# Output products of the context rows moved into the last attention units of a two-layer transformer kernel

## The chip, the core and the metric

The kernel runs on one core of one Trainium2 chip. The metric is device microseconds of one launch, as the median of several runs. Five engines work side by side, each through its own instruction list in order: PE (matrix products and transposes; PEld is its weight load), DVE (vector), ACT (scalar functions), POOL (a second vector engine) and SP, which here only issues DMAs. They wait for one another by semaphores.

## The reference, cut to what matters

Two layers over 1024 tokens and 256 context rows, width 1024. The change touches the end of the first (even) layer: the differential attention B, the gates, the output product with its residual, and the normalised input of the second layer.

```python
qa, ka, va, qb, kb, vb, g = _split(h @ w_in, EVEN_SPLITS)          # tokens; the context likewise from hc
ya = _window_gqa_sink(...)                                          # attention A, done before stage B
s = einsum('bqhte,bkhte->bhtqk', q, k) * e ** -0.5                  # attention B, 4 heads, two score maps t
p = softmax(s); a = p[:, :, 0] - lam * p[:, :, 1]
yb = rmsnorm(einsum('bhqk,bkhe->bqhe', a, v), b_subln_g) * (1.0 - lam_init)
y = concatenate([ya, yb], -1) * silu(g)
x = x + gate * (y @ w_out)                                          # 1024 token rows
xc = xc + gate_c * (yc @ w_out)                                     # 256 context rows, same w_out
h, gate = _modulate(x, ...); hc, gate_c = _modulate(xc, ...)        # second layer starts with a norm of each row
```

## The kernel before

Every product of activations and weights is made of three matmuls (`mm3`, L304 to L306): both operands are split into a high and a low part, and high x high, high x low and low x high are summed in PSUM. Splitting a tile is a rounding copy on ACT (the high part) and a subtraction on DVE or POOL (the low part, L214 and L218).

Stage B (`mark("B")` up to `mark("outE")`) has 20 units: 4 heads, and in each head five pairs of 128-row query blocks, the context pair (8, 9) first and then four token pairs. I number them 0 to 19; units 0, 5, 10 and 15 are the short context ones. A unit has three parts. `b_scores`: score matmuls (L906, into `sps`), their evacuation on DVE with a running minimum (L407), the exponential on ACT (L914), and the mix of the two score maps, on POOL for the first row block (L924 and the sums) and on DVE for the second (L927). `b_values`: transposes of the mixed maps (L955), a split on ACT and DVE (`phb`, `plb`), and products with V (L418 to L420). `b_norm`: after every second token unit a transposed RMS norm of the head's output (L977 to L1002) and, at a head's end, a store to DRAM (`ote`, L1000 and L1005).

`pipeline` lays these steps out at positions in units (values about 1.7 units after their scores, norms about 2.3 to 2.7) and between steps lets a filler emit other work: per unit of position the filler may emit `FILL_B` = 5.0 "us" of it, by the numbers that the filler's generator yields. That generator is `gates()`: eight gate projections (`gate_proj`: 12.8 us of yields each, PE products of `hE` with `whi` and `wlo`, a tanh on ACT and ten DVE steps, L396 and L398, then a store `gte`), and then the split of the eight 128-row tiles of the output weights (`fill_out_weights`, L847 to L855, 5.0 each; `woraw` is the loaded tile, with two buffers, `woE` the split weights). These tiles lie where `hE` and the gates' buffers lay, so they begin when the gates are done. What is left after the last unit is emitted by `fill.drain()`. Within reach, a list scheduler then orders the instructions of each engine, so the emission order is the frame and not the last word.

Stage outE goes over ten row blocks, context blocks 8 and 9 first, then 0 to 7. For each, `y_get` loads attention output and gate (`o_in`, `g_in`, three buffers each), multiplies and splits them (`yh`, `yl`); `out_half` makes 24 matmuls for each half of the columns and then two DVE steps, times the gate row (`t_o`, L1036) and plus the residual (`xn`, L1037). Each pair of blocks is normalised (`norm_rows`), and one block later transposed into the second layer's input `hO` (`emit_h`). The gate row `gate_e` has one buffer: the context's is loaded for blocks 8 and 9, the tokens' for the rest.

Of the kernel before, what the change touches and what calls it, by code (L numbers as in the profile page):

```python
# [9 lines left out]
F32 = mybir.dt.float32  # L10
# [22 lines left out]
SM_N = 332  # L33
FILL_A, FILL_B, FILL_D, FILL_M = 5.0, 5.0, 4.3, 5.0
S_BUFS_A, S_BUFS_B, S_BUFS_D, S_BUFS_M, K_BUFS_B, Q_BUFS_B = 11, 7, 12, 6, 1, 3
# [7 lines left out]
WO_RAW, Y_BUFS = 1, 3  # L43
Q_BUFS_D, WO_V, WO_Y, YL_V = 2, 2, 5.0, 1
POOL_MIX, POOL_Q = (0,), (8,)
# [51 lines left out]
def body(nc, tc, I, out, dbg=None):  # L97
# [82 lines left out]
    def f32(ap):  # L180
        return ap.bitcast(F32)
# [661 lines left out]

    def fill_out_weights(rp, wo, src, bufs=2):
        for kt in range(NK):
            raw = rp.tile([P, D], F32, tag="wada", name="woraw", bufs=bufs)
            SY.dma_start(raw, src[:, kt * D:(kt + 1) * D])  # L847
            for c in range(2):
                cs_ = slice(c * 512, (c + 1) * 512)
                A.copy(wo[c][0][:, kt], raw[:, cs_])  # L850
                eng = V if WO_V and kt % WO_V == c else G
                tt(eng, wo[c][1][:, kt], raw[:, cs_], f32(wo[c][0][:, kt]), ALU.subtract)
            yield WO_Y

# [3 lines left out]
    def y_part(t, src, gsrc, half, b):  # L858
        op, (yh, yl) = t
        ks = slice(4 * half, 4 * half + 4)  # L860
        bs = slice(b * P, (b + 1) * P)
        o, g = (op.tile([P, 4, P], F32, tag=x, name=x, bufs=Y_BUFS) for x in ("o_in", "g_in"))
        SY.dma_start(o, src[half][:, :, bs].rearrange("k p t -> p k t"))
        SY.dma_start(g, gsrc[half][:, :, bs].rearrange("k p t -> p k t"))
        V.scalar_tensor_tensor(o, o, 0.5, g, ALU.mult, ALU.mult)
        A.copy(yh[:, ks], o)  # L866
        tt(V if YL_V and half == YL_V - 1 else G, yl[:, ks], o, f32(yh[:, ks]), ALU.subtract)


# [3 lines left out]
    with ExitStack() as st:  # L873
# [134 lines left out]
        def gates():  # L1008
            with ExitStack() as gs:
                gp = pool(gs, "gateE", 2, side="right")  # L1010
                yield from items([w_item(W, [I["w_e"][18 + i]], lambda w, i=i: gate_proj(
                    gp, w, h, CHUNKS, GTE[i // 4][i % 4], T, True)) for i in range(8)])
            hE.close()
            with ExitStack() as gs:
                wo_box.append(out_weights(stW, "woE", "right"))
                wo_box.append(pool(stW, "yE", 1, side="right"))
                ad = pool(gs, "adaE", 2, side="right")
                yield from fill_out_weights(ad, wo_box[0], I["w_out_e"])

# [6 lines left out]
        fill.drain()  # L1026
    wo, yp = wo_box


    def out_half(op, y, wo, x, gate, xn, c, kts):  # L1030
        cs_ = slice(c * 512, (c + 1) * 512)
        ps = mm_ps()
        for i, kt in enumerate(kts):
            mm3(ps, y[1][0][:, kt], y[1][1][:, kt], wo[c][0][:, kt], wo[c][1][:, kt], i == 0, i == NK - 1)
        t = op.tile([P, 512], F32, tag="t", name="t_o")
        V.tensor_tensor(t, ps, gate[:, cs_], ALU.mult)  # L1036
        V.tensor_tensor(xn[:, cs_], x[:, cs_], t, ALU.add)  # L1037

# [7 lines left out]
    with ExitStack() as st:  # L1046
        op = pool(st, "outE", 1, side="left")
        kts = list(range(NK))

        def y_get(b):  # L1050
            t = y_load(yp)
            for half in range(2):
                y_part(t, OTE, GTE, half, b)
            return t

        order = [8, 9] + list(range(8))
        ys = {8: y_get(8)}
        gate = None
        late = []

        def emit_h(blocks, xns):
            run(h_cols(op, xns, 1, 1 if blocks[0] == 8 else 0, blocks[0] * P, h2, width=256))

        for gi in range(0, 10, 2):
            blocks, xns, x_in = order[gi:gi + 2], [], []
            if gi in (0, 2):
                gate = op.tile([P, D], F32, tag="gate", name="gate_e", bufs=1)
                gate_load(gate, 1 if gi == 0 else 0)
            for i, b in enumerate(blocks):
                xn = op.tile([P, D], F32, tag="xn", name="xn", bufs=3)  # L1070
                SY.dma_start(xn, I["x_o"][b * P:(b + 1) * P] if b < 8 else I["ctx"][(b - 8) * P:(b - 7) * P])
                nb = order[gi + i + 1] if gi + i + 1 < 10 else None
                if nb is not None:
                    ys[nb] = y_get(nb)
                else:
                    w_kd0 = Wp.load([I["w_o"][3]])
                y = ys.pop(b)
                for c in range(2):
                    out_half(op, y, wo, xn, gate, xn, c, kts)
                    if late and c == EMIT_C:  # L1080
                        emit_h(*late.pop(0))
                if b < 8:
                    SY.dma_start(X1[b], xn)
                xns.append(xn)
            norm_rows(op, xns)
            late.append((blocks, xns))
# [418 lines left out]
    with ExitStack() as st:  # L1505
# [14 lines left out]
        for b in range(8):  # L1520
# [8 lines left out]
            for c in range(2):  # L1529
                out_half(op, y, wo, x, gate2, xn, c, kts)  # L1530
                junk = op.tile([P, 512], BF16, tag="junk", name="junk2", bufs=2)
# [82 lines left out]
```

## Time and profile before

| what | us |
|---|---|
| median of 3 runs (lowest, highest) | 1668.4 (1663.4, 1669.59) |
| the profiled execution's own time | 1664.82 |
| its span | 1663.0 |
| PE busy in the span | 1582.6 (95%) |
| DVE busy | 1085.4 (65%) |
| ACT busy | 777.3 (47%) |
| POOL busy | 540.3 (32%) |

The profiled execution lies 1.8 us above its span and 3.6 us below the median. PE's busy time counts a matmul to its modelled end, so that neighbours overlap: how much work stands in a stretch is better counted from matmuls times the distance of their starts. The windows of the trace give busy time by stretch; I cut them where PE passes from one kind of work to the next: 478.9 us (scores of unit 0 done), 717.1 (of unit 16), 762.5 (of unit 19, the last), 822.7 (first transposes of normalised rows in outE) and 910.6 (first product of the second layer).

### The profile page before, as it was taken

The numbers are of one execution on the slowest core, as the hardware profiler recorded it, in microseconds if no ns is written. First come the engines' busy times: TensorE is split into PE (matmuls) and PEld (weight loads), VectorE is DVE, ScalarE is ACT, GpSimd is POOL, SyncE is SP. The second block draws the span as 40 slices with busy tenths as digits, with TensorE's granted clock in tenths as the row PEclk, the third lists the DMA queues.
The fourth block names the chain that finished last, engine by engine and source line by source line (L and its number), as shares of the span: only waits on it lengthen the run. The fifth ranks groups of instructions, "written<-read, shape, count | busy, mean of one in ns | idle before, by whom it ended". The sixth has DMA issues, their size and how long they took to land. (4 is left out here: it accounts for less than half of the span.)

```text
span 1663.0 us, 26799 instructions
## 1 busy us (share of the span) xinstructions
PE 1582.6 (95%) x9266; PEld 1330.1 (80%) x9266; DVE 1085.4 (65%) x2954; ACT 777.3 (47%) x1580; POOL 540.3 (32%) x713
## 2 busy tenths in 40 slices
PE   6988999999998999998999998999999999999997
PEld 3676767888877878887687897989788887888886
DVE  4674128878759887888776456352777757666576
ACT  5443107766646655666323323222566646554321
POOL 0465025555534433333323203120333314322211
PEclk9999999999999999999999999999999999999999
DMA  7447663252253332223853514666855445321452
GB/s 294 172 124 256 223 213 105 83 159 81 76 203 101 112 102 99 90 90 117 247 164 133 171 45 134 192 203 210 211 166 166 137 130 183 101 77 64 140 190 83
DMA packets 147375, 242.99 MB, mean 146 GB/s; under 512 B 10252, under 2 KB 93096, under 8 KB 145064
## 3 DMA queue, kind: packets, MB, share of 16 engines
q1 hardware_dynamic: 142328, 227.91, 44.1%
q10 hardware_dynamic: 4576, 11.54, 1.8%
q0 software_dynamic: 336, 1.84, 0.3%
q8 instruction: 73, 1.20, 0.3%
q14 instruction: 62, 0.51, 0.1%
HBM read 163.50 MB, written 77.74 MB: 145 GB/s over the span
## 5 line engine op out<-in xcount | busy, mean ns | idle before, releaser
L304 PE MATMUL mmps<-hE,whi 128*128 128x512 f32 (+1 forms) x408 | 148.6, 364 | 1.2 <-DVE gg L396 1.2
L218 POOL TENSOR_TENSOR wlo<-wraw,whi 128x256 fp32r<-128x256 f32 x120 | 92.2, 803 | 173.0 <-ACT whi L251 173.0
L306 PE MATMUL mmps<-hE,wlo 128*128 128x512 f32 (+1 forms) x408 | 146.4, 359 | 0.0
L305 PE MATMUL mmps<-hE,whi 128*128 128x512 f32 (+1 forms) x408 | 146.1, 358 | 0.0
L914 ACT ACTIVATE sB_t<-sB_t,mB 128x1280 f32<-128x1280 f32 (+1 forms) x80 | 95.5, 1194 | 57.1 <-DVE sB_t L407 50.6
L906 PE MATMUL sps<-kb,qb 128*128 128x512 f32 (+1 forms) x416 | 107.9, 361 | 4.5 <-DMA kb<-kb 2.3
L924 POOL TENSOR_SCALAR sB_t<-sB_t,cB 128x256 f32<-128x256 f32 x84 | 38.7, 482 | 156.3 <-DVE cB L920 74.8
L1449 POOL TENSOR_SCALAR sM_t<-sM_t,sM 128x1280 f32<-128x1280 f32 x32 | 43.3, 1353 | 137.4 <-DVE sM L1448 106.4
L304 PEld LDWEIGHTS mmps<-hE,whi 128*128 128x128 f32 x408 | 77.3, 189 | 11.4 <-issue 2.1
L407 DVE TENSOR_SCALAR_CACHE_REDUCE sB_t<-sps,mB 128x512 f32<-128x512 f32 (+1 forms) x128 | 78.2, 612 | 12.5 <-PE sps L906 9.7
L306 PEld LDWEIGHTS mmps<-hE,wlo 128*128 128x128 f32 x408 | 77.2, 189 | 9.9 <-issue 0.8
L305 PEld LDWEIGHTS mmps<-hE,whi 128*128 128x128 f32 x408 | 77.2, 189 | 9.2 <-issue 0.8
L906 PEld LDWEIGHTS sps<-kb,qb 128*128 128x128 f32 x416 | 69.4, 191 | 16.9 <-DVE sB_t L407 5.9
L1347 POOL TENSOR_SCALAR sD_t<-sD_t,sD 128x640 f32<-128x640 f32 (+1 forms) x64 | 48.5, 780 | 90.0 <-DVE sD L1344 37.1
L218 POOL TENSOR_TENSOR rot<-rot,csE 128x256 f32<-128x256 f32 x52 | 41.3, 816 | 109.0 <-DVE rot L331 105.2
L305 PE MATMUL mmps<-hO,whi 128*128 128x512 f32 (+1 forms) x192 | 75.0, 390 | 1.7 <-POOL hO L214 1.6
L304 PE MATMUL mmps<-hO,whi 128*128 128x512 f32 (+1 forms) x192 | 75.5, 393 | 0.0
L306 PE MATMUL mmps<-hO,wlo 128*128 128x512 f32 (+1 forms) x192 | 74.4, 388 | 0.0
L784 ACT ACTIVATE sA_t<-sA_t,mA 128x640 f32<-128x640 f32 (+2 forms) x80 | 59.6, 745 | 31.8 <-DVE sA_t L407 29.2
L218 POOL TENSOR_TENSOR yl<-o_in,yh 128x256 fp32r<-128x256 f32 x36 | 34.0, 966 | 121.9 <-ACT yh L866 121.7
L221 ACT CAST phm<-tps 128x512 fp32r<-128x512 f32 x80 | 45.7, 584 | 51.6 <-PE tps L1476 51.3
L794 POOL TENSOR_SCALAR sA_t<-sA_t,eA 128x640 f32<-128x640 f32 (+2 forms) x80 | 56.1, 724 | 37.9 <-DVE eA L792 14.6
(437 smaller groups left out, 5208.1 us busy)
## 6 DMA issues: line engine op xcount, KB each, us to landing
wraw<-w_e SPq DMA_DIRECT2D x26, 512.0 KB
wada<-w_ada_e SPq DMA_DIRECT2D x24, 512.0 KB
wada<-w_ada_o SPq DMA_DIRECT2D x24, 512.0 KB
wraw<-w_o SPq DMA_DIRECT2D x22, 512.0 KB
qb<-qk SPq DMA_DIRECT2D x76, 128.0 KB
qd_t<-qd SPq DMA_DIRECT2D x32, 256.0 KB
qk<-hl SPq DMA_DIRECT2D x10, 512.0 KB
vb<-vh SPq DMA_DIRECT2D x10, 512.0 KB
```

Of the source, the lines that this page charges most:

```text
L218: eng.tensor_tensor(out_[:, cs_], a[:, cs_], b[:, cs_], op)
L221: A.copy(dst_hi, src)
L304: T_.matmul(ps, lh, rh, start=first, stop=False)
L305: T_.matmul(ps, lh, rl, start=False, stop=False)
L306: T_.matmul(ps, ll, rh, start=False, stop=last)
L407: V.tensor_scalar(dst, ps, -scale, prev, ALU.mult, ALU.min, accum_out=acc)
L784: A.activation(St[:, :nl + L], St[:, :nl + L], AF.Exp, bias=mx, scale=-1.0, accum_out=ssum[:, i:i + 1])
L794: G.tensor_scalar(Ps[i][:, :nl + L], Ps[i][:, :nl + L], e[:, i:i + 1], 1.0, ALU.mult, ALU.mult)
L906: T_.matmul(ps[:, :n], Q[:, t, hl, i * P:(i + 1) * P], K[:, t, c0:c0 + n], start=hl == 0, stop=hl == 1)
L914: A.activation(St[:, :ncol], St[:, :ncol], AF.Exp, bias=mx, scale=-1.0, accum_out=s0g[:, si:si + 1] if t == 0 else ssum)
L1347: G.tensor_scalar(Ps[i][:, :w_], Ps[i][:, :w_], ssum[:, i:i + 1], 1.0, ALU.mult, ALU.mult)
L1449: G.tensor_scalar(St, St, ssum, 1.0, ALU.mult, ALU.mult)
```

## The change

`FILL_B` goes from 5.0 to 6.0, so the gates are used up after fewer units. The output weights are yielded at 2.5 instead of 5.0 each (`WO_YE`), so they are emitted under the last units. The generator then goes on: it takes a pool `outC`, loads the context's gate row and residual rows, fetches `y` for blocks 8 and 9 and emits their four `out_half` (5.12 us of yields each). Stage outE keeps blocks 0 to 7 only, with the context rows' norm at its start. The gate row is still one buffer (tag `gate`), now in `outC`.

```diff
-FILL_A, FILL_B, FILL_D, FILL_M = 5.0, 5.0, 4.3, 5.0
+FILL_A, FILL_B, FILL_D, FILL_M = 5.0, 6.0, 4.3, 5.0
-Q_BUFS_D, WO_V, WO_Y, YL_V = 2, 2, 5.0, 1
+Q_BUFS_D, WO_V, WO_YE, WO_Y, YL_V = 2, 2, 2.5, 5.0, 1
...
+    def out_half(op, y, wo, x, gate, xn, c, kts):
+        cs_ = slice(c * 512, (c + 1) * 512)
+        ps = mm_ps()
+        for i, kt in enumerate(kts):
+            mm3(ps, y[1][0][:, kt], y[1][1][:, kt], wo[c][0][:, kt], wo[c][1][:, kt], i == 0, i == NK - 1)
+            if i % 2 and i < NK - 1:
+                yield 1.28
+        t = op.tile([P, 512], F32, tag="t", name="t_o")
+        V.tensor_tensor(t, ps, gate[:, cs_], ALU.mult)
+        V.tensor_tensor(xn[:, cs_], x[:, cs_], t, ALU.add)
+        yield 1.28
...
-                yield from fill_out_weights(ad, wo_box[0], I["w_out_e"])
+                yield from fill_out_weights(ad, wo_box[0], I["w_out_e"], us=WO_YE)
+            oc = pool(stW, "outC", 1, side="right")
+            gate = oc.tile([P, D], F32, tag="gate", name="gate_c")
+            gate_load(gate, 1)
+            ys, xc = {}, []
+            for i in range(2):
+                xc.append(oc.tile([P, D], F32, tag="xn", name=f"xc{i}", bufs=3))
+                SY.dma_start(xc[i], I["ctx"][i * P:(i + 1) * P])
+            for i in range(2):
+                ys[i] = y_get(wo_box[1], 8 + i)
+            yield 2.0
+            for i in range(2):
+                for c in range(2):
+                    yield from out_half(oc, ys[i], wo_box[0], xc[i], gate, xc[i], c, list(range(NK)))
+            wo_box.extend((oc, xc))
...
-        ys = {8: y_get(8)}
-        gate = None
-        late = []
+        ys = {0: y_get(yp, 0)}
+        norm_rows(op, xc)
+        late = [(order[:2], xc)]
...
-        for gi in range(0, 10, 2):
+        gate = oc.tile([P, D], F32, tag="gate", name="gate_e")
+        gate_load(gate, 0)
+        for gi in range(2, 10, 2):
```

PE's list around the last scores (`sps<-kb,qb`) of unit 19, before. `hE` are gate products, `phb` and `plb` products with V, `of` the norm's transposes.

```order
L304 MATMUL mmps<-hE_134,whi 128x512
L305 MATMUL mmps<-hE_135,whi 128x512
L306 MATMUL mmps<-hE_134,wlo 128x512
L906 MATMUL sps<-kb,qb 128x512 x4
L955 MATMUL tps<-consts,sB_t 128x128 x4
L906 MATMUL sps<-kb,qb 128x256 x2
L304 MATMUL mmps<-hE_134,whi 128x256
L305 MATMUL mmps<-hE_135,whi 128x256
```

The same list after the change, in unit 18; `woE` are output products, and the last gate product stands in unit 17.

```order
L304 MATMUL mmps<-woE_8297,yh 128x512
L305 MATMUL mmps<-woE_8298,yh 128x512
L304 MATMUL mmps<-woE_8295,yh 128x512
L924 MATMUL sps<-kb,qb 128x512 x2
L305 MATMUL mmps<-woE_8296,yh 128x512
L924 MATMUL sps<-kb,qb 128x256 x2
L306 MATMUL mmps<-woE_8297,yl 128x512
```

Of the 96 matmuls of the context rows, 18 stand ahead of the last scores and 78 behind them; before, all 96 stood behind, and 78 gate matmuls stood between the last scores of unit 16 and those of unit 19 where 6 stand now.

DVE's list before, behind the last scores' evacuation: the subtractions of the output weights (`woE<-woraw`) stand among the splits for the last products with V (`plb`) and those of block 8's `y`.

```order
L214 TENSOR_TENSOR woE_8835<-woraw,woE_8834 128x512
L214 TENSOR_TENSOR plb<-tps,phb 128x512 x2
L865 SCALAR_TENSOR_TENSOR o_in<-o_in,g_in 128x512
L214 TENSOR_TENSOR woE_8833<-woraw,woE_8832 128x512
L214 TENSOR_TENSOR yl<-o_in,yh 128x512
```

DVE's list after, from the fifth of these eight subtractions on: each now has score evacuations (`sB_t,mB<-sps`) behind it.

```order
L214 TENSOR_TENSOR woE_8298<-woraw,woE_8297 128x512
L200 SCALAR_TENSOR_TENSOR rst<-rst,evB 128x2
L407 TENSOR_SCALAR sB_t,mB<-sps,mB 128x256
L201 SCALAR_TENSOR_TENSOR rsy<-rst,rsy 128x2
L214 TENSOR_TENSOR yl<-o_in,yh 128x512
L199 TENSOR_TENSOR rst<-rsy 128x2
L407 TENSOR_SCALAR sB_t,mB<-sps 128x512
```

All eight subtractions now stand in units 17 to 19.

On POOL, whose list takes the mixes of the units' first row blocks in turn, all 16 pieces of the weights' subtractions stood behind the last mix before; now six stand between the mixes of units 16 and 17, four between those of 17 and 18, six between those of 18 and 19.

## Rows read from the trace of the kernel before

**Rows 1.** The page's first line: the span of the profiled execution.

```profile
span 1663.0 us, 26799 instructions
```

**Rows 2.** Windows: busy us (x count) of PE, PEld, DVE, ACT, POOL; clock, DMA, GB/s.

```profile
478.90:717.10 238.20, 225.95 (x1400) 193.04 (x1399) 201.44 (x648) 145.08 (x287) 93.56 (x156) 0.99 0.32 103
717.10:762.50 45.40, 44.41 (x279) 38.67 (x278) 39.36 (x135) 28.50 (x55) 15.05 (x27) 1.00 0.16 53
762.50:822.70 60.20, 51.90 (x277) 41.90 (x277) 45.22 (x93) 27.23 (x60) 24.75 (x31) 1.00 0.74 225
822.70:910.60 87.90, 85.30 (x402) 68.38 (x401) 64.77 (x136) 31.32 (x59) 26.40 (x32) 1.00 0.46 152
...
478.90:539.40 60.50, 54.05 (x326) 45.00 (x325) 57.13 (x186) 38.54 (x76) 27.12 (x46) 0.98 0.35 106
539.40:717.10 177.70, 171.90 (x1076) 148.04 (x1076) 144.30 (x463) 106.55 (x212) 66.44 (x110) 1.00 0.31 101
```

**Rows 3.** Waits, 479 to 717 us: who waited for whom: total, times, longest.

```profile
PE sps L906 <- DMA kb<-kb: 2.3, 1, 2.3
...
DVE sB_t L407 <- PE sps L906: 14.3, 23, 1.0
```

**Rows 4.** Timeline of PE: start us, us, engine, line, tiles, [idle before, releaser].

```profile
764.85 0.63 PE L955 MATMUL tps<-consts,sB_t 128*128 128x128 f32 x4
765.24 0.36 PE L304 MATMUL mmps<-hE,whi 128*128 128x256 f32 x1
...
765.55 0.28 PE L306 MATMUL mmps<-hE,wlo 128*128 128x256 f32 x1
765.67 0.28 PE L418 MATMUL pvps<-phb,vbt 128*128 128x256 f32 x1
...
804.60 0.39 PE L304 MATMUL sps<-woE,yh 128*128 128x512 f32 x1
804.83 0.39 PE L305 MATMUL sps<-woE,yh 128*128 128x512 f32 x1
```

**Rows 5.** Timeline of PE behind the last scores: one of its waits.

```profile
770.92 0.63 PE L955 MATMUL tps<-consts,sB_t 128*128 128x128 f32 x4 [2.70 <-DVE plb L214]
```

**Rows 6.** Groups by line, 717.1 to 762.5 us: busy us, mean ns | idle before.

```profile
L396 DVE SCALAR_TENSOR_TENSOR gg<-th,mmps 128x128 f32<-128x128 f32 x8 | 2.0, 279 | 0.7 <-ACT th L390 0.7
```

**Rows 7.** Tile woraw: duration ns min/median/max, first and last start us.

```profile
L850 ACT CAST woE<-woraw x16: 609/620/624, 772.8 to 797.7; 128x512 fp32r<-128x512 f32 x16
L218 POOL TENSOR_TENSOR woE<-woraw,woE x16: 724/736/1193, 774.1 to 798.6; 128x256 fp32r<-128x256 f32 x16
...
L214 DVE TENSOR_TENSOR woE<-woraw,woE x8: 681/692/1212, 773.5 to 799.1; 128x512 fp32r<-128x512 f32 x8
```

**Rows 8.** Timeline of DVE and POOL while the weights are split.

```profile
789.93 0.65 DVE L200 SCALAR_TENSOR_TENSOR rst<-rst,evB 128x4 f32<-128x4 f32 x1
...
791.99 0.16 DVE L200 SCALAR_TENSOR_TENSOR rst<-rst,evB 128x4 f32<-128x4 f32 x1
...
789.15 1.42 POOL L218 TENSOR_TENSOR yl<-o_in,yh 128x256 fp32r<-128x256 f32 x2
```

**Rows 9.** Timeline of SP, ACT and DVE: a load and its use; the last store.

```profile
775.50 0.33 SPq L847 DMA_DIRECT2D woraw<-w_out_e  x1
...
779.15 0.62 ACT L850 CAST woE<-woraw 128x512 fp32r<-128x512 f32 x1 [1.61 <-DMA woraw<-w_out_e]
...
795.67 0.36 ACTq L1005 DMA_DIRECT2D ote<-ob  x1
...
801.99 0.38 SPq L863 DMA_DIRECT2D o_in<-ote  x1
```

**Rows 10.** Timeline of DVE in outE, and PE's waits from 822 to 911 us.

```profile
820.64 0.69 DVE L1036 TENSOR_TENSOR t_o<-sps,gate_e 128x512 f32<-128x512 f32 x1 [1.40 <-DMA gate_e<-grow]
...
PE tps L485 <- DVE hf L493: 2.6, 4, 0.9
```

More of the change, by code (lines that the diff above doesn't have):

```diff
@@ L842, in out_weights, with fill_out_weights @@
         return [[p_.tile([P, NK, 512], F32R, name=f"{name}{c}{i}") for i in range(2)] for c in (1, 0)][::-1]
-    def fill_out_weights(rp, wo, src, bufs=2):
+    def fill_out_weights(rp, wo, src, bufs=2, us=WO_Y):
         for kt in range(NK):
@@ L852, in fill_out_weights @@
                 tt(eng, wo[c][1][:, kt], raw[:, cs_], f32(wo[c][0][:, kt]), ALU.subtract)
-            yield WO_Y
+            yield us
     def y_load(op):
@@ L867, in y_part, with y_get @@
         tt(V if YL_V and half == YL_V - 1 else G, yl[:, ks], o, f32(yh[:, ks]), ALU.subtract)
+    def out_half(op, y, wo, x, gate, xn, c, kts):
[9 more added lines that the diff above has]
+        yield 1.28
+    def y_get(p_, b):
+        t = y_load(p_)
+        for half in range(2):
+            y_part(t, OTE, GTE, half, b)
+        return t
     mark("B")
@@ L1026, in body @@
         fill.drain()
[L1027 to L1037, printed above, removed]
+    wo, yp, oc, xc = wo_box
     mark("outE")
@@ L1048, in body @@
         kts = list(range(NK))
[L1050 to L1054, printed above, removed]
         order = [8, 9] + list(range(8))
-        ys = {8: y_get(8)}
-        gate = None
-        late = []
+        ys = {0: y_get(yp, 0)}
+        norm_rows(op, xc)
+        late = [(order[:2], xc)]
         def emit_h(blocks, xns):
             run(h_cols(op, xns, 1, 1 if blocks[0] == 8 else 0, blocks[0] * P, h2, width=256))
-        for gi in range(0, 10, 2):
[L1065 to L1068, printed above, removed]
+        gate = oc.tile([P, D], F32, tag="gate", name="gate_e")
+        gate_load(gate, 0)
+        for gi in range(2, 10, 2):
+            blocks, xns = order[gi:gi + 2], []
             for i, b in enumerate(blocks):
-                xn = op.tile([P, D], F32, tag="xn", name="xn", bufs=3)
-                SY.dma_start(xn, I["x_o"][b * P:(b + 1) * P] if b < 8 else I["ctx"][(b - 8) * P:(b - 7) * P])
+                xn = oc.tile([P, D], F32, tag="xn", name="xn", bufs=3)
+                SY.dma_start(xn, I["x_o"][b * P:(b + 1) * P])
                 nb = order[gi + i + 1] if gi + i + 1 < 10 else None
                 if nb is not None:
-                    ys[nb] = y_get(nb)
+                    ys[nb] = y_get(yp, nb)
                 else:
@@ L1078, in body @@
                 for c in range(2):
-                    out_half(op, y, wo, xn, gate, xn, c, kts)
+                    run(out_half(oc, y, wo, xn, gate, xn, c, kts))
                     if late and c == EMIT_C:
                         emit_h(*late.pop(0))
-                if b < 8:
-                    SY.dma_start(X1[b], xn)
+                SY.dma_start(X1[b], xn)
                 xns.append(xn)
@@ L1529, in body @@
             for c in range(2):
-                out_half(op, y, wo, x, gate2, xn, c, kts)
+                run(out_half(op, y, wo, x, gate2, xn, c, kts))
                 junk = op.tile([P, 512], BF16, tag="junk", name="junk2", bufs=2)
```

## The prediction

> **What bounds the kernel now.** I read the windows first. The span is 1663.0 us [rows 1], and the change reaches from the second unit of stage B to the end of outE, 478.9 to 910.6 us: 431.7 us in four stretches [rows 2]. PE is shown busy nearly throughout, but that overlaps neighbours, so I count its work: a 512-column matmul starts 0.23 us after the one before, a 256-column one 0.12, four transposes take 0.39 [rows 4]; unrounded over longer runs 0.227, 0.120 and 0.098. Counted with the order lists, PE's work and what is missing to the stretch's length, its gap, are:
>
> - units 1 to 16 (238.2 us): 376 gate, 336 score, 378 V products and 308 transposes, 210.6 us, gap 27.6;
> - units 17 to 19 (45.4 us): 42.7, gap 2.7;
> - last scores to the first transposes of normalised rows (60.2 us): 47.9, gap 12.3;
> - the rest of outE (87.9 us): 82.6, gap 5.3.
>
> So PE bounds it, but 48 us in these 432 are lost, and only they can be won. The gap of 12.3 is what the change aims at: behind the last scores PE waits for the last units' splits, once 2.70 us [rows 5], while the weights are loaded and split by ACT, POOL and DVE [rows 7]. In units 1 to 5 (478.9 to 539.4) DVE is busy for 57.1 of 60.5 us: it sets that pace. In units 6 to 16 DVE has 144.3 of 177.7 and PE has 162.1 of work: PE sets it [rows 2], and DVE waits for scores, 14.3 us in 23 places, where PE's own largest wait is 2.3 us [rows 3].
>
> **The change, part by part.** No work is removed; it is moved between stretches whose bound differs.
>
> *Higher rate, units 1 to 16.* 54 gate matmuls of 512 columns and 42 of 256 come in here: 54 x 0.227 + 42 x 0.120 = 17.3 us more PE work, 227.9 in all. DVE gets 12 gate steps of 0.279 [rows 6] and one longer one, 3.7 us, and 205.1 in all. Of PE's extra work 3.3 us fall into units 1 to 5, which DVE bounds: 60.5 becomes some 62. The other 14.0 fall into units 6 to 16: 176.1 of work. Their gap was 15.6. If it stays, 191.7; the nearest row for PE that is kept fed is the stretch of units 17 to 19, gap 2.7 of 45.4 or 6%, which makes 10.6; at the low end half of that is left, some 6. I take 11: 187. Sum 249 for 238.2, with 243 and 254 as ends. So most of the 17.3 us of work is paid for here, and 6 us of gap are filled.
>
> *Units 17 to 19.* PE loses 54 + 18 gate matmuls here and gains 18 output products: 42.7 - 12.3 - 2.2 + 4.1 = 32.3 us. It no longer sets the pace. DVE was busy 39.4 of 45.4 [rows 2]; it loses 12 gate steps (3.4) and gains eight subtractions of weights at 0.692 [rows 7], and three steps for `y` of the same size: 7.6. That is 43.6. With the idle 6.0 us that it had, 49.6; I take 49. Low end 46, if it is held up less than before, since PE now has room. High end 54: the subtractions at their longest, 1.212 [rows 7], add 4. ACT gets 16 copies at 0.620 [rows 7], 9.9 us on 28.5, and POOL 11.8 on 15.0; both still have cover in 49 us. The queue on SP: the loads of unit 19's queries stand behind the first three loads of weights. The third waits until the first tile is split; but unit 19's scores come some 25 us later, so that costs nothing unless the splits are late by that much.
>
> A row speaks against it: six small DVE steps beside POOL's additions took some 0.65 us each where the next took 0.16 [rows 8]. The Trainium skill has the rule for it (SBUF — State Buffer, section "Who interferes with whom"): a DVE instruction with two SBUF inputs and a POOL instruction that reads SBUF exclude each other, and the later one waits for the whole instruction. Some of those six steps have one input, so row and rule agree only in part. By the rule, 16 POOL pieces of 0.736 us among some 40 two-input DVE steps in 49 us would cost about 40 x 0.24 x 0.37 = 3.5 us, an estimate, and the sum would be 1671; by the rows it lies between 46 and 54.
>
> *Behind the last scores.* PE has 47.9 - 2.9 (24 gate matmuls) - 4.1 (18 output products) - 0.3 (three transposes, now behind the mark) = 40.6 us of work. The waits on weights are gone: all their splits are done. New is that block 0's second half can wait. It needs the last head's stored output, and only 35 products, 7.9 us, stand between the last norm's transposes and its first matmul; before, the context rows covered this. The path is: the copy out (about 0.7), the store, the load, DVE's product and ACT's copy (0.7 and 0.6). A load from issue to use took 3.65 us (775.50 to 779.15); the store, issued at 795.67, let the next load go at 801.99, 6.3 us later [rows 9]. So 9.3 with a store as short as a load, or 12.0: a wait of 1.4 to 4.1. I take 3 and add 2 for the last units' short waits: gap 5 (2 to 10) for 12.3. The stretch: 45.6 us for 60.2.
>
> *The rest of outE.* Before, the gate row was reloaded here, and DVE stood 1.40 us for it; soon after, PE waited 2.6 us on DVE's `hf` in four places [rows 10]. Now the row is loaded when block 9 is done, while PE works on block 0. The buffer is still one, and the load stands on SP ahead of the one for block 0's second half, but that one waits longer, for the store. I take 0.9 off: 87.0 (85.5 to 88).
>
> Sum: 249 + 49 + 45.6 + 87.0 = 430.6 for 431.7: 1.1 us faster. From the profiled execution's own time, 1664.8, that is 1663.7; it lies 3.6 below the median, so on the median's footing 1668.4 - 1.1 = 1667.3. The gap does not vanish: some 14 us of it go, half behind the scores and half in the early units, and 14 come back in units 17 to 19, where PE has lost its filling to DVE. Everything behind 910.6 keeps its order but for a few rows, and costs nothing.
>
> **The rivals.**
>
> *PE alone becomes the bound (faster).* The fuller rate hides every small wait: units 6 to 16 at 182 (-5), units 17 to 19 at 46 (-3), the gap behind the scores at 2 (-3). That is 11 off, 1656. For it: DVE, ACT and POOL have slack in units 6 to 16. Against it: units 1 to 5 are DVE's already, and three units without gates must then run at DVE's pace with hardly any idle time.
>
> *The weights' loads pace the last units (slower).* There are two raw buffers; DVE's subtractions stand in its list ahead of evacuations of scores, and some of POOL's behind unit 18's mix. If a tile's load starts only when POOL has let go of the buffer, DVE stands for load and copy, 3.65 + 0.62 us [rows 7, 9], with the scores queued behind it, PE behind these. Three tiles (the sixth to eighth) can meet this; at 3.6 each it is 11 us, 1678. It decides if DVE reaches a subtraction less than 4.3 us after the buffer came free. Against it: about 7 to 8 us of DVE work stand between the steps that free a buffer and those that want its next tile, except for the seventh, where I count 4.5.
>
> *The change doesn't do what it says (no difference).* Only 18 of the 96 products stand ahead of the last scores. If these 18 wait for `yl` or for POOL's halves, weaving wins nothing, and block 0's second half is left without cover: gap 10 behind the scores, 1672.
>
> **How the numbers follow.** Forecast 0.52, PE alone 0.24, weights' loads 0.16, no weaving 0.08. A measurement here can tell about 0.5%, 8.3 us. Faster than 1660: the first rival and a little of the forecast, 0.25. Slower than 1676.7: the second and a little of the rest, 0.18. Within: 0.57. All low ends together give 1654, all high ones 1681; leaving out a tenth on each side, 1656 to 1679. The likeliest is 1667.
>
> **What would show it.** In the profile after: unit 16's scores end some 11 us later than before (728), unit 19's at 777, the first transposes at 822 to 823, the second layer's first product at 909 to 910. In units 17 to 19 PE's work should fill two thirds of the time and DVE nine tenths. The PE waits on `woE` should be gone, and one on `yh` of block 0 should appear. I am wrong in the first term if unit 16 ends before 723 or after 733; in the second if DVE is idle for over 8 us there, or waits for a load of `woraw`; in the third if a wait of over 5 us stands ahead of block 0's second half.

## The result, and the profile after

The changed kernel takes 1678.8 us (median of 6 runs, 1673.5 to 1682.8) against 1668.1 (1663.4 to 1669.6): ratio 1.0062, interval 1.0041 to 1.0083. It is 10.7 us slower, where I had said 1 us faster. The profiled execution is 1681.4 us, with this first line, which answers [rows 1]:

```profile
span 1679.6 us, 26787 instructions
```

The windows of the profile after, cut at the same events as [rows 2] (unit 0's, 16's and 19's last score matmul, the first transposes of normalised rows, the second layer's first product; columns as there):

```profile
481.30:735.70 254.40, 243.68 (x1497) 209.87 (x1496) 201.29 (x661) 145.50 (x291) 92.62 (x157) 0.99 0.31 97
735.70:790.80 55.10, 43.13 (x223) 33.63 (x223) 46.91 (x134) 35.34 (x68) 27.22 (x41) 0.85 0.55 172
790.80:842.40 51.60, 46.36 (x237) 37.91 (x237) 34.89 (x81) 18.41 (x43) 14.09 (x17) 0.93 0.36 108
842.40:930.00 87.60, 85.26 (x402) 68.41 (x401) 65.11 (x136) 31.39 (x59) 26.16 (x32) 1.00 0.48 159
```

Read the first column of numbers behind the window, then the clock. Units 1 to 16 take 16.2 us more than before, units 17 to 19 take 9.7 more, the stretch behind gives back 8.6, the rest of outE 0.3. The clock, 1.00 in three of the four stretches before, stands at 0.85 and 0.93 in the two where the matrix work was thinned out. (Between the two profiled executions lie 16.6 us: 17.0 in these four stretches, 2.4 ahead of them, where no edit reaches, and -2.8 behind them; by the medians it is 10.7.)

In units 17 to 19 this is what PE, and then DVE, waited for:

```profile
PE sps L924 <- DVE sB_t L407: 7.6, 6, 3.3
...
DVE sB_t L407 <- POOL sB_t L218: 4.0, 2, 3.7
DVE sB_t L407 <- PE sps L924: 1.9, 3, 1.3
```

PE waits for DVE to evacuate scores, and DVE for POOL's mix to free a score tile. Five of PE's six waits of over 2 us from unit 6 to outE, on the timeline (the sixth, of 2.10 us at 762.4, is for DVE's `rsi`):

```profile
571.10 0.55 PE L418 MATMUL pvps<-phb,vbt 128*128 128x256 f32 x1 [4.06 <-DMA vbt<-vb]
...
743.25 0.50 PE L924 MATMUL sps<-kb,qb 128*128 128x256 f32 x2 [2.47 <-DVE sB_t L407]
...
773.28 1.22 PE L924 MATMUL sps<-kb,qb 128*128 128x512 f32 x2 [3.29 <-DVE sB_t L407]
...
797.90 0.50 PE L306 MATMUL mmps<-woE,yl 128*128 128x512 f32 x1 [2.99 <-POOL yl L218]
...
834.90 0.50 PE L304 MATMUL sps<-woE,yh 128*128 128x512 f32 x1 [2.02 <-ACT yh L866]
```

Each of these five has a spell of half clock (1.2 GHz) beside it in the clock's records: from 570.5 for 6.8 us, 744.5 for 10.2, 771.8 for 6.8, 799.2 for 3.4 and 836.7 for 3.4. That is 30.6 us of spells between unit 0 and the second layer, against 3.4 before. DVE's work, in the windows, grew from 39.4 to 46.9 us in units 17 to 19, and its idle time from 6.0 to 8.2.

To take the stretches apart I count, for each, PE's work at full clock (the pitches of the prediction), the extra time of matmuls that started in a half-clock spell, and the remaining gap. The cuts from here on are at the start of the last score evacuation instead of the last score matmul, so they lie up to 3 us later:

```
                 before: length work half gap   after: length work half gap
units 1 to 16            238.0 210.4  1.5 32.0          254.6 228.2  2.8 29.4
units 17 to 19            47.2  44.6  0.0  4.0           57.2  34.4  5.8 18.2
behind, to transposes     58.3  45.4  0.0 13.5           48.9  37.8  3.1  8.5
rest of outE              87.8  82.5  0.0  7.3           87.5  82.5  0.0  7.0
```

(The three add up to more than the length, by 6 us in units 1 to 16 and by 1 to 2 elsewhere, before and after alike, since some matmuls start closer than the pitch: the differences count.) The 17.8 us of work that came into units 1 to 16 are paid there nearly in full, with 16.6. The two stretches that lost them took 105.5 us together before and take 106.1 now: 17.8 us of work went out, and 9.2 us of gap and 8.9 of half clock came in.

### The profile page after: what moved, and what is told of

It reads as the page before. It is cut to its first block, busy times and chain, and to the rows that moved or that the text cites. A ratio compares the mean times of both kernels' runs of the same rounds, so it can differ in the third digit from the quotient of the medians.

```text
span 1679.6 us, 26787 instructions
## 1 busy us (share of the span) xinstructions
PE 1595.1 (95%) x9266; PEld 1339.2 (80%) x9266; DVE 1083.9 (65%) x2954; ACT 775.6 (46%) x1580; POOL 541.1 (32%) x713
## 5 line engine op out<-in xcount | busy, mean ns | idle before, releaser
L924 PE MATMUL sps<-kb,qb 128*128 128x512 f32 (+1 forms) x416 | 114.2, 376 | 11.3 <-DVE sB_t L407 8.3
L1464 POOL TENSOR_SCALAR sM_t<-sM_t,sM 128x1280 f32<-128x1280 f32 x32 | 43.2, 1350 | 138.2 <-DVE sM L1463 106.7
L304 PEld LDWEIGHTS mmps<-hE,whi 128*128 128x128 f32 x408 | 77.4, 190 | 10.8 <-issue 2.1
L221 ACT CAST phb<-tps 128x512 fp32r<-128x512 f32 x84 | 48.8, 582 | 49.4 <-PE tps L973 48.2
L221 ACT CAST phm<-tps 128x512 fp32r<-128x512 f32 x80 | 45.6, 583 | 51.7 <-PE tps L1491 51.4
```

The source lines that it names most:

```text
L221: A.copy(dst_hi, src)
L304: T_.matmul(ps, lh, rh, start=first, stop=False)
L924: T_.matmul(ps[:, :n], Q[:, t, hl, i * P:(i + 1) * P], K[:, t, c0:c0 + n], start=hl == 0, stop=hl == 1)
L1464: G.tensor_scalar(St, St, ssum, 1.0, ALU.mult, ALU.mult)
```

## The experiments

Each was timed beside the kernel before on the same chip, and ratios are to that. The lengths of all of them stand in a table at the end of this section; they come from one profiled execution each, which lay between 6.3 us under its kernel's median (all halves on DVE, the fastest of ten) and 4.5 over it (stores on ACT, the slowest of ten).

**The rate alone.** The kernel before with `FILL_B` at 6.0.

```diff
-FILL_A, FILL_B, FILL_D, FILL_M = 5.0, 5.0, 4.3, 5.0
+FILL_A, FILL_B, FILL_D, FILL_M = 5.0, 6.0, 4.3, 5.0
```

> The kernel before with FILL_B = 6.0 alone: gates denser, output weights split under the last units at 5.0 each, no context products woven in. If the denser gates are the harm (a load of V in unit 6 that SP issues behind a gate store and a weight load, PE waiting 4.1 us for it, then 6.8 us at half clock; units 17 to 19 without gates), it is slower than the kernel before by 8 to 12 us, like the whole change. If the woven products and the split weights are the harm, it lies within 4 us of the kernel before.

1677.6 us, ratio 1.0055 (1.0032 to 1.0078), with as much half clock, 30.6 us. So the rate alone makes nearly the whole loss. It brings the splits with it: as the gates end early, seven of DVE's eight stand in units 17 to 19 here too. What the woven products add to it is within the noise.

**The rest alone.** The changed kernel with `FILL_B` back at 5.0.

> The changed kernel with FILL_B = 5.0: context products and weights in the generator, but gates at the old rate, so that they last to the end of unit 19. If the rate is the harm, this is within 4 us of the kernel before (1664 to 1672) and the granted clock in units 17 to 19 is 1.00 again. If the weaving is the harm, it stays slower by 6 or more.

1673.6 us, ratio 1.0023 (1.0008 to 1.0038), by the medians between the two results that I had named. Units 17 to 19 are back at 47.2 us, clock 1.00; but now all splits, and the context rows' products, stand behind unit 19, and that stretch takes 64.1 for 58.3. Weaving wins nothing here either.

**The clock.** Each score matmul of units 17 to 19 made twice into the same bank, so that PE has work there.

```diff
+                        for _ in range(REP if hd == 3 and grp[0] in (2, 4, 6) else 1):
-                        for hl in range(2):
+                            for hl in range(2):
```

> The changed kernel with every score matmul of units 17 to 19 made twice into the same bank (the second pair overwrites the first): 72 more matmuls, some 13.8 us more PE work at the full clock, no more DVE, ACT or POOL work. Theory A (after the change PE idles in units 17 to 19, its granted clock falls to half there, 0.85 on the mean of that stretch, and what follows a wait runs at half speed): more PE work keeps the clock up; the granted clock of the stretch from unit 16's to unit 19's last scores rises to 0.95 or more and the time stays within 3 us of the changed kernel or falls by up to 6. Rival B (the stretch is DVE's and POOL's, and the clock is only a sign of it): clock as before or better, time higher by 3 to 10, since each score comes later.

1680.1 us, ratio 1.0075 (1.0046 to 1.0103). Half clock falls from 30.6 to 13.6 us, gap and half-clock time in units 17 to 19 from 24.0 to 11.7, but the doubled work takes their place: 54.9 us.

```profile
733.60:788.50 54.90, 50.58 (x292) 42.87 (x292) 49.79 (x140) 38.52 (x78) 29.88 (x44) 0.94 0.60 182
```

The clock is 0.94, just short of the 0.95 that I had named, and DVE is now busy for 49.8 of the 54.9 us. So a higher clock, bought with work on the scores' own path, wins no time here. (The doubling also lets the scheduler order these units' lists anew, so it is not the clock alone that differs.)

**The queue on SP, first part.** The gates' stores on ACT's queue.

```diff
-        SY.dma_start(dst, g)
+        A.dma_start(dst, g)
```

> The changed kernel with the gates' stores issued by ACT's queue and not by SP's, so that the loads of V, queries and weights no longer stand behind a store that waits for DVE's last gate step. If the load of V in unit 6 (4.06 us of PE wait and 6.8 us at half clock behind it) is worth what it shows, 4 to 8 us faster than the changed kernel: 1671 to 1675. If that wait is taken up by later slack, within 3 us of it.

1673.0 us, ratio 1.0025 (1.0008 to 1.0042): 5.8 us won by the medians, but not where I had looked. Units 1 to 16 stay at 254.2, and PE still waits 3.15 us for V. The stretch behind unit 19 falls from 48.9 to 44.6. In the changed kernel the last gate store stood on SP between loads of weights, and the context rows' loads of the gates behind more of these, which wait for a raw buffer:

```profile
736.53 0.58 SPq L847 DMA_DIRECT2D woraw<-w_out_e  x1
737.55 0.33 SPq L400 DMA_DIRECT2D gte<-gg  x1
738.05 5.76 SPq L847 DMA_DIRECT2D woraw<-w_out_e  x2
...
751.26 0.35 SPq L847 DMA_DIRECT2D woraw<-w_out_e  x1
751.65 8.83 SPq L864 DMA_DIRECT2D g_in<-gte  x3
```

PE's wait for POOL's `yl`, 2.99 us above, is 0.4 there.

**The queue on SP, second part.** V loads of heads 1 to 3 on ACT's queue, and both moves together.

```diff
-                VBt[hd] = bp.tile([P, 10, 2, P], F32R, tag="V", name="vbt", bufs=1)
-                SY.dma_start(f32(VBt[hd]), VB[:, hd])
+                v_load(hd)
...
+            if grp[0] == 6 and hd < 3:
+                v_load(hd + 1, A)
```

> The changed kernel with the V loads of heads 1 to 3 issued on ScalarE's queue, in the place where the last products of the head before are written, so that they no longer stand behind the gates' weight load and store on SyncE's queue. Theory 1 (that queue costs the units 1 to 16 the wait of 4.06 us ahead of unit 6's products and the half clock of 6.8 us behind it): no wait on the V load, no half clock near 571 us, the stretch of units 1 to 16 falls from 254.6 to 247 to 250 us, the total by 4 to 7 us to about 1673. Theory 2 (the wait is replaced by another, since VectorE is nearly as busy as TensorE there): the stretch stays within 2 us of 254.6 and the total within 2 us of 1678.8.

> The changed kernel with both queue moves at its own rate of 6: gates' stores and V loads on ScalarE's queue. If the two moves act on different waits, the total is about 1668 to 1670 (5.8 us from the stores, as measured, and some 4 from the V loads); if they are the same wait, it is 1672 to 1674. The stretch of units 17 to 19 should stay at 55 to 57 us in either case, as no V load waits there.

1686.5 us (1.0093) and 1677.7 (1.0046): by the ratios 5 and 3.5 us worse than without the move. The wait on V fell to 1.5 us, yet units 1 to 16 kept 252.7 and 254.4, so a shorter wait did not shorten them.

That does not clear the load, though. At rate 6 a 512 KB load of gate weights (`wraw`) is issued 1.2 us ahead of the V load of head 1, in all twelve kernels; at the lower rates nothing is issued in the twelve us ahead of it. V's last part lands 8.0 to 10.1 us after issue in eleven of the twelve and 6.0 in one, against 5.7 to 6.8 in the eight kernels at lower rates. Eight kernels at rate 6 have the same rows up to unit 16's end, and there units 1 to 16 go with that landing, from 247.3 us where it took 6.0 to 255.2 where it took 9.7 (correlation 0.94). Neither queue move touched the weights' load; a run that moves it was not made, so this is not shown.

**The splits.** First I only wrote them behind all units.

```diff
+                yield 1e6
                 yield from fill_out_weights(ad, wo_box[0], I["w_out_e"], us=WO_YE)
```

> The changed kernel with the splits of the output weights, and the context rows' products behind them, held back until all 20 units are written; the gates keep the rate of 6. What is read: the stretch from the last score evacuation of unit 16 to that of unit 19 (47.2 us before, 57.2 us changed; TensorE's gap in it 4.0 us before and 18.2 changed, by start-to-start pitches at full clock). Theory 1 (the splits' 5.7 us on VectorE and 12.3 us on GpSimd lie on the chain that frees score tiles there): the stretch falls to about 47, the one behind it grows from 48.9 to about 60, the total stays within 3 us of the changed kernel. Theory 2 (without the gates' products the units lack matrix work whatever VectorE carries, each wait is one of latency from score to evacuation to mix, and the low clock follows): the stretch stays at 54 or more, and the total grows by 8 us or more over the changed kernel, to about 1687.

1682.0 us (1.0060), and no test: the scheduler still put seven of DVE's eight splits ahead of the last evacuation. It serves as a second sample of the changed kernel (1.0062). Then I held them with a true dependence, and combined that with the doubled scores.

```diff
             raw = rp.tile([P, D], F32, tag="wada", name="woraw", bufs=bufs)
+            if after and kt < bufs:
+                V.tensor_copy(raw[:, :1], after[0][:, :1])
```

> The changed kernel with the splits truly held back: the first two raw weight buffers are written with one column of unit 19's last row of minima before their loads, so that no load and no split of the output weights can start before unit 19's last evacuation (holding them back in the written order alone had not moved them). Gates at a rate of 6. Read: unit 16's last evacuation to unit 19's. Theory 1 (the splits' 5.7 us on VectorE and 12.3 us on GpSimd make the units long): 47 to 49 us, TensorE's gap about 10 of them. Theory 2 (units without the gates' products have no work to cover the chain score, evacuation, exponential, mix, and the granted clock falls in the holes): 54 to 57 us, gap 18 to 20, as in the changed kernel. In both the stretch behind grows to 58 or more and the total to 1685 or more under theory 2, to 1678 under theory 1.

> The same held splits, and each score matmul of units 17 to 19 made twice into the same bank, so that these units have about as much matrix work (44.6 us) as in the kernel before, where they took 47.2 us, and no splits. With the two runs before it this fills a table: matrix work yes or no, splits yes or no (no, yes 57.2; yes, yes 54.9). Theory 1 (splits): 47 to 48 us here. Theory 2 (independent matrix work): doubled scores give work, but not work that is free of the evacuations, since a second score matmul waits for the same bank as the first; the stretch stays at 52 or more. If splits and work count alike, it is about 49 to 51.

1687.1 us (1.0112) and 1678.6 (1.0070). Their units 17 to 19:

```profile
736.90:787.80 50.90, 39.46 (x220) 30.24 (x219) 40.07 (x132) 29.25 (x59) 15.38 (x28) 0.90 0.27 84
```

```profile
733.40:779.70 46.30, 45.34 (x284) 38.94 (x283) 42.30 (x133) 30.55 (x61) 17.85 (x31) 1.00 0.36 109
```

So the table is: thin work with splits 57.2, without 50.9; doubled work with splits 54.9, without 46.3. The splits, and the context rows' first products that went with them, cost 6 to 9 us in these units; thin work costs 2 to 5, at least, since doubled scores also stand in the scores' own way. Without splits DVE is busy for only 40.1 of the 50.9 us, and with doubled scores for 42.3 of the 46.3: in thin units it stands and waits. But held back the splits lengthen the stretch behind by 10 to 13 us (61.6 and 59.5 against 48.9 and 49.3). With thin work it was worth its price to have them under the units (1.0062 against 1.0112); with doubled scores it made no difference (1.0075 against 1.0070).

Read along its other side, the table says something of the clock. With the splits held, the same useless work won 8.4 us by the medians, 1687.1 to 1678.6, and each of its six runs was shorter than any of the other four; units 17 to 19 fell by 4.6 us and their clock rose from 0.90 to 1.00. With the splits in place, where DVE is busy for 49.8 of 54.9 us, it won nothing. How much of the 8.4 us is the clock's and how much the new order's is not shown.

**Which engine carries the splits.** All low halves on DVE, or all on POOL.

```diff
-                eng = V if WO_V and kt % WO_V == c else G
+                eng = V if us == WO_YE or kt % WO_V == c else G
```

> The changed kernel with all 16 low halves of the output weights of this stage on VectorE, none on GpSimd. If GpSimd carries the loss (its pieces stand ahead of the mixes that free score tiles, and slow VectorE's small operations beside them): units 17 to 19 fall from 57.2 to 50 to 53 us although VectorE gets some 5.7 us more, and VectorE's wait for a mix (4.0 us) is gone. If VectorE carries it: the stretch grows to 60 to 63 us, and the total to about 1682 to 1685.

> The changed kernel with all 16 low halves on GpSimd (32 pieces, some 24 us by 0.79 us for one), none on VectorE. If VectorE carries the loss: units 17 to 19 fall from 57.2 to about 51 us. If GpSimd carries it: the wait for mixes grows above 4.0 us and the stretch to 60 us or more. GpSimd's own work in the stretch would be 43 of 57 us.

1674.3 us (1.0026) and 1680.0 (1.0049). With DVE alone the units took 50.2 us, with POOL alone 56.2, and this looked like the answer. (The 50.2 come from that kernel's fastest execution of ten, and units 1 to 16, whose rows are the changed kernel's, took 247.3 in it.) Of small DVE steps, the group in the changed kernel and then in the kernel with all halves on DVE (columns as in [rows 6], over units 17 to 19):

```profile
L200 DVE SCALAR_TENSOR_TENSOR rst<-rst,evB 128x4 f32<-128x4 f32 (+1 forms) x6 | 2.5, 412 | 0.0
L938 DVE SCALAR_TENSOR_TENSOR cB<-cB,nlam,s0g 128x1 f32<-128x1 f32 x6 | 2.4, 400 | 0.0
```

```profile
L200 DVE SCALAR_TENSOR_TENSOR rst<-rst,evB 128x4 f32<-128x4 f32 (+1 forms) x6 | 0.9, 156 | 0.0
L938 DVE SCALAR_TENSOR_TENSOR cB<-cB,nlam,s0g 128x1 f32<-128x1 f32 x6 | 1.3, 214 | 0.0
```

The steps are back at their old length (0.155 and 0.215 us before) without POOL's pieces. That part holds. But the next run takes the conclusion away.

**Rates with these edits.** Rate 5.4 or 5.2 with both queue moves; then 5.4 with all halves on DVE and the stores moved, with the V loads moved too, and with neither queue move; last the third of these five at rates 6 and 5.0.

> The changed kernel with both queue moves (gates' stores and V loads on ScalarE's queue) and the fill rate at 5.4 in place of 6, which ends the gates some way into unit 19 rather than ahead of unit 17. If the loss is made where units run without gates (theory 1), few units do here: units 17 to 19 take 47 to 50 us, units 1 to 16 about 242 to 245, the total is 1666 to 1670, at the kernel before. If the loss goes with the splits and products being moved at all (theory 2), the total stays above 1673.

> Rate 5.2 with gates' stores and V loads on ScalarE's queue, the rest as changed. Between the measured 5.0 (1673.6 us, without the queue moves) and 5.4 (1667.6). If only the units that run without gates cost, it is 1664 to 1668, since nearly none do; units 1 to 16 about 240 to 242, units 17 to 19 47 to 48, the stretch behind 56 to 59. If the gain of 5.4 was a matter of chance between programs, it lies at 1668 to 1673.

> Rate 5.4, all low halves of this stage's output weights on VectorE, the gates' stores on ScalarE's queue. If the two causes found add (gates ending too early, 1667.6 at 5.4; the GpSimd pieces, 4.5 us at rate 6), the total is 1662 to 1666, under the kernel before by 0.2 to 0.4%. If few pieces stand in units 17 to 19 at 5.4 anyway, it is 1666 to 1670.

> The same with the V loads of heads 1 to 3 on ScalarE's queue too. At the rate 6 this move cost 4 us against the stores' move alone (1677.7 against 1673.0); if that was the move's doing, it is 4 us over the run before it, if it was chance between programs, it is within 2 us.

> Rate 5.4 and all low halves on VectorE, no queue move. If the stores on SyncE's queue cost what the rate 6 showed (5.8 us), it is about 1668 to 1671; if not, it is within 2 us of the first run of these three.

> Rate 6 with both edits (all low halves on VectorE, gates' stores on ScalarE's queue). If the edits add, as at 5.4 (4.5 us and 5.8 us off the changed kernel's loss of 10.7), the total is level with the kernel before, within 2 us, and the rate is worth the 8 us between this and 5.4. If the rate matters less once GpSimd is out of the way, it is 0.2 to 0.5% faster than before. Units 17 to 19 should take 49 to 51 us.

> Rate 5.0 with both edits. The gates end behind unit 19, so no split stands in units 17 to 19 (47 us) and all of them stand behind (59 to 62 us, as with rate 5.0 and the rest as changed, 64.1). If the gain of 5.4 is that splits and gates share the last units, this is level with the kernel before or up to 3 us slower; if the gain is only that the splits left GpSimd, it is 0.3 to 0.5% faster than before.

5.4 gave 0.9990 and 5.2 gave 1.0031. The next three gave **0.9950 (0.9932 to 0.9967)**, 0.9986 and 0.9977: the first, 1656.5 us against 1664.5, beats both kernels. At rate 6 the same code gave 1.0062, at 5.0 1.0088. These two and 5.2 missed what I had expected: 5.2 came out where I had put chance between programs, and 5.0, expected at most 3 us slower, lost nearly 15. At rate 6, with no split on POOL, units 17 to 19 took 58.6 us:

```profile
740.40:799.00 58.60, 46.24 (x244) 35.52 (x242) 51.23 (x148) 38.73 (x80) 20.19 (x31) 0.85 0.55 167
```

against 50.2 with the same halves on DVE and the stores on SP. In this one ACT waited for loads of weights, with exponentials queued behind the copies, more than twice as long as in the changed kernel (or with the stores on SP, 3.4 us):

```profile
ACT woE L850 <- DMA woraw<-w_out_e: 7.8, 5, 2.8
```

```profile
ACT woE L850 <- DMA woraw<-w_out_e: 3.5, 3, 1.9
```

(first at rate 6 with both edits, then the changed kernel). So the engine that carries the splits' 6 to 9 us is not settled. A third raw buffer would tell and was not tried.

The kernel at 5.4 that beats both, over the first three stretches:

```profile
483.70:722.40 238.70, 231.11 (x1442) 197.78 (x1442) 200.25 (x652) 144.31 (x287) 95.35 (x158) 1.00 0.32 103
722.40:773.90 51.50, 46.24 (x290) 38.68 (x288) 45.16 (x147) 34.83 (x74) 18.73 (x32) 1.00 0.39 122
773.90:820.80 46.90, 44.43 (x218) 36.05 (x219) 36.01 (x85) 18.71 (x39) 9.35 (x9) 0.96 0.59 187
```

Its clock in units 17 to 19 is 1.00. Its last gate product stands in unit 18, at 750.1 us, and half of the weights' copies behind unit 19's last evacuation. Units 1 to 16 took in 7.2 us of PE's work here and grew by only 0.7. Of the 6.4 us that its profile gains on the kernel before, the four stretches that the edits touch make 5.1; 4.3 are lost ahead of them, and 5.6 won behind, where hardly a row changes.

All runs, with the lengths of the first three stretches and the half-clock spells in the four:

```
kernel                                   rate ratio   1-16  17-19 behind  half clock
before                                   5.0  1       238.0  47.2   58.3    3.4
changed                                  6.0  1.0062  254.6  57.2   48.9   30.6
before, rate alone (e2)                  6.0  1.0055  254.6  58.9   52.3   30.6
stores on ACT (e4)                       6.0  1.0025  254.2  56.4   44.6   20.4
splits written later, not moved (e5)     6.0  1.0060  255.1  56.4   48.8   23.8
V loads on ACT (e6)                      6.0  1.0093  252.7  58.6   46.8   20.4
both queue moves (e8)                    6.0  1.0046  254.4  58.8   43.4   23.8
scores doubled (e1)                      6.0  1.0075  251.4  54.9   49.3   13.6
splits held (e9)                         6.0  1.0112  252.3  50.9   61.6   23.8
splits held, scores doubled (e10)        6.0  1.0070  253.6  46.3   59.5   13.6
halves on DVE (e12)                      6.0  1.0026  247.3  50.2   48.3   10.2
halves on POOL (e13)                     6.0  1.0049  255.2  56.2   46.0   27.2
halves on DVE, stores on ACT (e17)       6.0  1.0062  253.9  58.6   45.3   27.2
both queue moves (e7)                    5.4  0.9990  243.1  49.3   53.4   13.6
halves on DVE (e16)                      5.4  0.9977  237.3  52.8   52.9   10.2
halves on DVE, stores on ACT (e14)       5.4  0.9950  238.7  51.5   46.9    3.4
the same, V loads on ACT (e15)           5.4  0.9986  242.6  53.0   49.2   10.2
both queue moves (e11)                   5.2  1.0031  243.6  51.9   62.1   23.9
changed but for the rate (e3)            5.0  1.0023  239.6  47.2   64.1   13.6
halves on DVE, stores on ACT (e18)       5.0  1.0088  245.9  51.6   68.6   27.2
```

Three pairs differ by the rate alone, 6 against 5.4: 1.0046 and 0.9990, 1.0026 and 0.9977, 1.0062 and 0.9950. The rate costs 0.5 to 1.1% each time. At 6, with splits in place, units 1 to 16 take 247 to 255 us, at 5.4 237 to 243, with 10.5 us of work between them, while units 17 to 19 and the stretch behind take 98 to 111 us together at 6 and 98 to 106 at 5.4, with all that more work in them. No half clock falls into units 17 to 19 at 5.4.

The other edits do not add up. By the medians the stores' move won 5.8 us at rate 6 and 5.6 at 5.4, and lost 4.3 at rate 6 with the halves on DVE. Single profiles of one order differ too, in units 1 to 16 by 7.9 us over the eight kernels with the same rows, so a difference of that size in one row of the table is no finding by itself.

## Why the prediction was wrong, step by step

The failed step is the balance of the gaps: "some 14 us of it go, half behind the scores and half in the early units, and 14 come back in units 17 to 19". By the table of gaps, with the time lost at half clock counted in, 1.3 us went in the early units, 1.9 behind the scores, and 20.0 came in units 17 to 19. So units 17 to 19 and the stretch behind, which were to shrink from 105.6 to 94.6 us, stayed at 106.7, and three terms of the sum came out too low by nearly the same amount, 5 to 6 us each in the profile. The measured 1678.8 lies just inside the range of 1656 to 1679; that is owed to the range's width, since the direction was wrong.

- **Units 1 to 16, forecast 249 (243 to 254), measured 254.4.** Just outside its ends, and unit 16's scores ended at 735.7, past the 733 that I had named as the sign of being wrong (2.4 us of that come from ahead of stage B). PE's work was counted rightly (228 us). Units 1 to 5 took 60.2, where I had 62; the miss is in units 6 to 16, 194.2 for 187. The gap was to shrink by 6.6 us, from 27.6 to 21, as "PE that is kept fed" loses less; it shrank by 2.6, and half clock took 1.3 of that back. The row chosen for it, units 17 to 19 with 2.7, was not a near one. I had not priced the queue on SP: the V load that PE waited 4.06 us for stands there behind a gates' store and a load of gate weights. Moving the store, or V itself, changed little; in the one execution where V landed in 6.0 us, the same rows took 247.3, inside the forecast.
- **Units 17 to 19, forecast 49 (46 to 54), measured 55.1.** Outside its ends. DVE's sum was 3.3 us short, 46.9 us busy where I had 43.6, because its small steps took longer (the next point); and I let it run without idle beyond its old 6.0 us. It stood 8.2 of 55.1, just over the 8 that I had named as the sign of being wrong, and the two waits above show on what: mixes and scores. So more of the miss is DVE's work than its waits. That units without independent PE work also run into the latency of the chain score, evacuation, exponential, mix is seen where the splits were held: DVE stood 10.8 us of 50.9 there. I had measured that chain only with cover.
- **POOL beside DVE.** The Trainium skill (SBUF — State Buffer, "Who interferes with whom") has the rule that gave me an estimate of 3.5 us, which I weighed and left out of the sum. The three groups of small steps here, L200, L201 and L938, took 6.8 us against 3.1 before: 3.7 more. Trace and rule agree in size, and by the rule the forecast would have been nearer; but one step with a single input, L188, took 0.70 us too, where its other took 0.16.
- **Behind the last scores, forecast 45.6, measured 51.6.** The waits on weights are gone, as said, and block 0's second half waited 2.02 us, inside my 1.4 to 4.1. What I had not seen is `yl` behind POOL's mix, 2.99 us, and the half clock: 3.1 us of time, where I had none.
- **The rest of outE, forecast 87.0, measured 87.6.** Right.
- **The clock.** I left it out of the sum; the time that matmuls lost at half clock went from 1.5 to 11.7 us. How much of the loss goes with it can be read from the runs: over the 260 runs that have a clock on record, each compared with the mean of its kernel and chip, 0.001 of mean granted clock goes with 1.25 us (correlation -0.73). The kernel before has a mean of 0.9900, the changed one 0.9853: 5.9 us of the 10.7. This is a correlation, since a hole both costs time and lowers the clock; the doubled scores, which raise the clock with useless work, won nothing with the splits in place and 8.4 us with the splits held.
- **The rivals.** "PE alone becomes the bound" fell: the work went in, but the early units' gap closed by 2.6 us and that of units 17 to 19 opened by 14.2. "The weights' loads pace the last units" had the place and the size (1678), not the carrier: PE never waited for them there, ACT did for 3.5 us in three places, while DVE stood for mixes. That it named 1678 was luck. "Weaving wins nothing" came true in that one point: with the rate alone the loss was the same.

Open are three things: what makes V land late at rate 6, what holds units 17 to 19 and the stretch behind at about 100 us however much work they have, and why edits that help alone fail together. Behind the second layer's first product, where hardly a row changes, kernels differ by up to 9 us (744.2 to 753.5), and ahead of stage B by up to 6.5, which I can't explain. The intervals hold for runs of one program; how much of the smaller differences is chance between programs was not measured.

## What to carry to other kernels

Filler that runs out early can be paid twice: where it is moved to, since an engine that is already the bound may close few gaps with it (17.8 us of work cost 16.6 at rate 6, though 7.2 cost 0.7 in the best kernel), and again where it is missing, in waits and a lower clock. So try the rates between: here 5.4, with the gates ending in unit 18 and half of the splits behind unit 19, beat 5.0 and 6 with the same code. When a stretch loses its cover, the sum of the next busiest engine is only a floor: add what its small steps lose beside the other engines and the latency of its chain, and allow for the granted clock.

## What the runs showed of the hardware

- The granted clock fell to half beside PE waits of 2.0 to 4.1 us, and stayed there 3.4 to 10.2 us: five waits of 14.8 us in all with 11.7 us lost by the matmuls that ran at half clock. The 2.70 us wait of [rows 5] and the one of 2.10 us for `rsi` brought no such spell. The Trainium skill (TensorE: Matmul & The Clock Gate, "Part 1: The HAM clock gate") says that the throttled clock is the default and activity releases it; the trace agrees in kind, with 0.85 in units of thin work and 1.00 with the doubled scores and held splits.
- Small DVE steps of 0.155 us took 0.41 beside POOL's two-input pieces, and 0.156 once these were gone; DVE's own eight further subtractions did not lengthen the units in that execution, its kernel's fastest.
- The same V load landed its 16 parts 5.3 to 10.1 us after issue in one execution, and 5.1 to 6.0 in another whose rows up to there are the same; a 512 KB load was issued 1.2 us ahead of it in both. Without one it ended at 5.7 to 6.8 us in eight kernels.
